# Two of four output-projection column blocks as one Strassen pass in a one-core hybrid decoder layer

## The chip, the cores and the metric

The kernel runs on one core of a Trainium2 chip. The metric is the device time of one execution in microseconds (us), lower is better. The engines are named as in the profile: PE (TensorE matmul), PEld (its weight loads), DVE (VectorE), ACT (ScalarE), POOL (GpSimd) and SP (SyncE, which here only issues DMAs). PE reads operands from SBUF and accumulates in PSUM, which has eight banks of 128 x 512 fp32.

## The reference

One decoder layer over 512 tokens of width 2048, in fp32:

```python
h = rmsnorm(x, ln_mix)
sb_q, sb_k, sb_v, sw_q, sw_k, sw_v = split(h @ w_in)
sb_o = stick_breaking_attention(sb_q, sb_k, sb_v)               # 16 heads of 64
sw_o = sliding_window_sink_attention(sw_q, sw_k, sw_v, sinks)   # 16 heads, 4 key/value heads
mixed = concat([rmsnorm(sb_o, sb_out_norm), rmsnorm(sw_o, swa_out_norm)])
x = x + mixed @ w_out                                           # 2048 x 2048
h = rmsnorm(x, ln_ffn)
gate, up = split(h @ w_gate_up)                                 # 2048 x 11264
x = x + (silu(gate) * up) @ w_down                              # 5632 x 2048
return rmsnorm(x, ln_final)
```

The change concerns the second half of `mixed @ w_out`: the 1024 columns of `sw_o`, normed, times the lower 1024 rows of `w_out`, which is 1024 x 2048.

## The kernel before

**A product in fp32.** PE multiplies in the type fp32r, so each fp32 operand is split in two: a head (`hi`, the value rounded by an ACT copy) and a rest (`lo`, value minus head, a DVE or POOL subtraction). A product is three matmuls: head x head, head x rest, rest x head. Weights come by DMA into `raw` tiles (512 KB, three buffers, `wp`), ACT makes `whi` and DVE `wlo`, two buffers each.

**The slab queue.** Plain products wait in a list, `queue`. An entry is a slab of weights with the steps that use it; a step is one trio of matmuls (128 x 128 weights, 512 columns each in the output projection). `step()` runs the next one; at the third step of a slab it asks for the loads of the next two slabs and the split of the next one (`split`, L205). `pull(ns)` runs steps for a nominal time, `drain(mark)` runs them up to a place in the queue, and `defer(n, fn)` calls `fn` after `n` steps. `add_tok` (L370) queues a product with tokens on the output partitions: four slabs of 256 rows, each with 2 x 4 steps, into four PSUM banks, one for each of four token tiles.

**The Strassen passes.** `Block` (L490) does a 2 x 2 block product with seven products instead of eight, in the order `PD`. Each product has two parts of 256 rows, and one part (a slot) is 12 matmuls of 512 columns (`product`, L508). The sums on the weight side are POOL subtractions (`difference`), the sums on the left side are `form`s. For a slot, ACT makes the head twice: `hi` in SBUF for PE, and `hp` in PSUM, which DVE reads to make `lo`. `take` (L523) adds a finished bank into the accumulators on DVE. What is done in which slot stands in a table, `plan`, filled by `at_slot(n, stage, fn)` and emptied by `run(n, stage)`. `ValuePass` (L598) does the projection of `sb_v` in this way in 28 slots, with a prologue in slots -6 to -1 that runs beside the last steps of an earlier product. The feed-forward part uses the same scheme.

**Order.** Engines take their instructions in the order in which the planner of the language emits them: mostly program order, with unpinned instructions moved where the planner finds a gap. `pV`, `pA`, `pG`, `pT` and `dma` are pinned, that is, they keep program order. An instruction waits by semaphores for what it reads and for the buffers that it writes.

**Around the change.** The sliding-window stage (L1069 to L1180) runs 16 jobs (four head groups of four token blocks): scores, exponentials, transposes (`swa_tr`), and the product with the values (`swa_av`). Its PE work is mixed with steps of the queue, which holds the last input projections and then `add_outA(0..3)`, the first half of the output projection. At the last block of a group, `swa_av` squares the outputs `oB` on ACT and POOL adds them into `sqB` (L1153). `drain()` (L1181) empties the queue; `sumsq_rstd` (L732) makes `rstdB`, the factor of each token. Then `add_outB(0..3)` (L1258) queues the second half: four column blocks of 512, each 32 steps, into banks `four(1)`, which are the two `m` banks and the two `o` banks. Its left side is `mixB`, made by `mix_split` (L1040), which scales `oB` by the norm weight (`gcol`) and splits it. At the end of a block, `done` adds the bank times `rstdB` into `x2[c]`, stores it, and defers `h2_split(c)` (L1199): 16 PE transposes and the scaling of the feed-forward's input `xh`. After block 1 all seven `form`s of the first half of `xh` are made in one deferred call (L1269), on DVE, ACT and, for one sum, POOL. The feed-forward part starts with `start_unit` (L1726), which makes the forms of the second half.

Of the kernel before, what the change touches and what calls it, by code (L numbers as in the profile page):

```python
# [37 lines left out]
def tile_hymba(ctx: ExitStack, tc: tile.TileContext, x, ln_mix, w_in, sb_norm, swa_norm,  # L38
# [39 lines left out]
    def po():  # L78
        return bank("o", 2)
# [645 lines left out]
    def sumsq_add(acc, o, first, t):  # L725
        if first:
            A.activation(out=acc, in_=o, func=AF.Square)
        else:
            A.activation(out=t, in_=o, func=AF.Square)  # L729
            G.tensor_tensor(out=acc, in0=acc, in1=t, op=ALU.add)  # L730

    def sumsq_rstd(acc, name):  # L732
        pb = po()
        for t in range(NT):
            mm(pb[:, 2 * t:2 * t + 2], lhsT=acc[:, t * P:(t + 1) * P], rhs=ones[:, 0:2],
               start=(t == 0), stop=True, skip_group_check=True)
# [265 lines left out]
    sqB = swp.tile([P, 512], F32, name="sqB", bufs=1)
    oB = [swp.tile([P, 4, 512], F32, tag="oB", name="oB", bufs=2) for _ in range(2)]
# [135 lines left out]
    def swa_av(g, blk):  # L1139
        B = blks[(g, blk)]  # L1140
        nk = B.nk
        ob = pz()
        for j in range(nk):
            vb = swv[0][:, blk - nk + 1 + j, g, :]
            mm(ob, lhsT=vb, rhs=B.p[j][0], start=(j == 0), stop=False)
            mm(ob, lhsT=vb, rhs=B.p[j][1], start=False, stop=(j == nk - 1))
# [12 lines left out]
    pull(2600.0)  # L1159
    at(swa_scores, 0)  # L1160
    stacks = {0: lambda: stack_queries(1, 0), 1: lambda: stack_queries(1, 1), 2: lambda: stack_keys(0, 1),
              5: lambda: stack_keys(1, 0), 6: lambda: stack_keys(1, 1)}
    for j in range(NJ + 2):
        at(swa_exp, j)
        if j == 3:
            rstdA = sumsq_rstd(sqA, "rstdA")
        if j in stacks:
            stacks[j]()
        pull(SWFILL / 4)
        at(swa_tr, j - 1)  # L1170
        pull(SWFILL / 4)
# [5 lines left out]
        pull(SWFILL / 4)  # L1177
        at(swa_norm, j)
        at(swa_scores, j + 1)
        pull(SWFILL / 4)  # L1180
# [45 lines left out]
    def form(p, s, parts="+hl"):  # L1226


        eV, eA = (pV, pA) if s and p not in "17" else (V, A)
        xa, xb = xh[2 * s], xh[2 * s + 1]  # L1230
        a11, a21 = xa[:, :, 0:256], xa[:, :, 256:512]
        if p not in "17":
            a12, a22 = xb[:, :, 0:256], xb[:, :, 256:512]
        if "+" in parts:
            if p == "7":
                src = e8("s3")[:, 0:2, :].rearrange("p u (a b) -> p (u a) b", a=2)
                V.tensor_tensor(out=src, in0=a11, in1=a21, op=ALU.subtract)
            elif p == "5":
                src = a21
                eV.tensor_tensor(out=src, in0=a21, in1=a22, op=ALU.add)  # L1240
            elif p == "6":
                src = a11
                eV.tensor_tensor(out=src, in0=a21, in1=a11, op=ALU.subtract)
            elif p == "3":
                src = a12
                (pG if s else G).tensor_tensor(out=src, in0=a12, in1=a11, op=ALU.subtract)
            else:
                src = {"1": lambda: a11, "2": lambda: a12, "4": lambda: a22}[p]()
            fsrc[p, s] = src
        src = fsrc[p, s]  # L1250
        if "h" in parts:
            hc[p, s] = form_tile(p, s)
            eA.activation(out=hc[p, s][:, :, 0:256], in_=src, func=AF.Copy)
        if "l" in parts:
            hl = hc[p, s]
            eV.tensor_tensor(out=hl[:, :, 256:512], in0=src, in1=f(hl)[:, :, 0:256], op=ALU.subtract)

    def add_outB(c):  # L1258
        def done(t, pb):
            xc = x2[c][:, t, :]  # L1260
            V.scalar_tensor_tensor(out=xc, in0=pb, scalar=rstdB[:, t:t + 1], in1=xc, op0=ALU.mult, op1=ALU.add)
            if t == NT - 1:
                if c < 3:
                    dma(out=x2s[c], in_=x2[c])
                    defer(6, lambda: h2_split(c))
                else:
                    nc.scalar.dma_start(out=x2s[c], in_=x2[c])
                if c == 1:
                    defer(12, lambda: [form(p, 0) for p in PR])  # L1269
                if c == 2:  # L1270
                    defer(12, lambda: [form(p, 1) for p in "17"])
            if c < 3:
                A.activation(out=junk, in_=xc, func=AF.Square, accum_out=ss2[:, t, c:c + 1])
# [12 lines left out]
    r2 = {}

# [585 lines left out]
```

## Time and profile before

| what | value |
|---|---|
| median of 3 runs | 1988.39 us (1988.22 to 1989.09) |
| the profiled execution | 1988.84 us |
| its span (first to last instruction) | 1987.0 us |
| instructions | 28973 |
| DVE, ACT, POOL busy | 1480.3, 1498.5, 999.8 us |
| queue of SP: bytes, share of 16 DMA engines | 244.11 MB, 42.2% |
| HBM, mean over the span | 120 GB/s |

A page of the profile gives the busy time of each engine. Other views give the chain of work that ended last, groups of instructions by line, the instructions of one engine in order of time, and the busy time in chosen stretches. In a row of the timeline the first number is the start in us from the span's start, the second the duration, "x4" the number of merged instructions, and a bracket at the end the idle time of the engine before it with what ended it. The end of a matmul is modelled, so that consecutive matmuls overlap in these rows; their pace is seen from start to start. The 1.84 us between span and time lie outside the instructions.

### The profile page before, as it was taken

How to read it: one execution, taken by the hardware profiler on the slowest of the kernel's cores; microseconds unless marked ns; L12 is line 12 of the kernel's file. 1: busy time of each engine (PE TensorE's matmuls, PEld its weight loads, DVE VectorE, ACT ScalarE, POOL GpSimd, SP SyncE). 2: the span in 40 equal slices, each digit the busy share in tenths (PEclk: the TensorE clock that was granted, in tenths of full speed). 3: DMA queues.
4: the chain of work that ended last, by engine and by line, in shares of the span. 5: the costliest groups of instructions: out<-in, count | busy, mean ns of one | idle time of the engine just before them, and what ended most of it. 6: DMA issues, size and time to landing. Idle time of an engine off the chain costs nothing.

```text
span 1987.0 us, 28973 instructions
## 1 busy us (share of the span) xinstructions
PE 1974.1 (99%) x10204; PEld 1687.7 (85%) x10204; DVE 1480.3 (75%) x2053; ACT 1498.5 (75%) x2015; POOL 999.8 (50%) x441
## 2 busy tenths in 40 slices
PE   9999999999999999999999999999999999999998
PEld 8888888898888888888888888888888888888886
DVE  6676888889964787777777777777777867767767
ACT  6775878868753587777777777777777788888887
POOL 2840000000010266657576666657575778878883
PEclk9999999999999999999999999999999999999999
DMA  6415454422342554444545354444534734433523
GB/s 203 148 54 142 97 144 113 121 75 85 96 138 96 172 136 113 127 125 114 137 103 144 101 139 110 129 121 118 135 104 129 279 127 148 149 127 120 177 75 117
DMA packets 290977, 252.81 MB, mean 127 GB/s; under 512 B 12560, under 2 KB 234832, under 8 KB 288400
## 3 DMA queue, kind: packets, MB, share of 16 engines
q1 hardware_dynamic: 289072, 244.11, 42.2%
q0 software_dynamic: 1376, 5.52, 0.9%
q8 instruction: 81, 1.33, 0.3%
q10 hardware_dynamic: 384, 1.34, 0.2%
q14 instruction: 64, 0.52, 0.1%
HBM read 218.40 MB, written 19.92 MB: 120 GB/s over the span
## 4 chain that ended last, share of the span: by engine, by line
PE 97%; ACT 2%; DVE 1%; issue 0%; DVEq 0%; POOL 0%; ACTq 0%; POOLq 0%
PE o L118 36%; PE m L118 30%; PE m L418 3%; PE m L419 3%; PE m L420 3%; PE m L384 2%; PE m L382 2%; PE m L383 2%; PE z L118 1%; PE o L384 1%; PE o L382 1%; PE o L383 1%; PE z L933 1%; PE o L961 1%; PE z L1132 1%; PE z L886 1%
## 5 line engine op out<-in xcount | busy, mean ns | idle before, releaser
L118 DVE TENSOR_TENSOR wlo<-t,hp 128x1024 fp32r<-128x1024 f32 x247 | 301.2, 1219 | 184.6 <-PE o L118 114.2
L118 POOL TENSOR_TENSOR t<-raw,t 128x1024 f32<-128x1024 f32 x111 | 282.2, 2543 | 281.5 <-ACT hp L118 269.6
L118 ACT ACTIVATE whi<-t 128x1024 fp32r<-128x1024 f32 x247 | 262.1, 1061 | 126.4 <-PE o L118 76.4
L118 PE MATMUL o<-hca,whi 128*128 128x512 f32 x880 | 307.5, 391 | 0.0
L118 POOL TENSOR_TENSOR t<-raw,raw 128x1024 f32<-128x1024 f32 x114 | 295.0, 2590 | 21.9 <-issue 11.3
L118 DVE TENSOR_TENSOR wlo<-raw,hp 128x1024 fp32r<-128x1024 f32 x187 | 228.3, 1221 | 93.2 <-issue 52.2
L118 ACT ACTIVATE whi<-raw 128x1024 fp32r<-128x1024 f32 (+1 forms) x189 | 200.0, 1058 | 105.0 <-PE m L118 75.0
L118 ACT ACTIVATE hp<-t 128x1024 fp32r<-128x1024 f32 x247 | 249.2, 1009 | 2.9 <-POOL t L118 2.9
L118 PE MATMUL o<-hca,wlo 128*128 128x256 f32 x880 | 244.0, 280 | 0.0
L118 ACT ACTIVATE hp<-raw 128x1024 fp32r<-128x1024 f32 x191 | 192.9, 1010 | 3.8 <-DVE wlo L118 1.4
L118 PEld LDWEIGHTS o<-hca,whi 128*128 128x128 f32 x880 | 164.2, 187 | 35.8
L118 PE MATMUL m<-hca,whi 128*128 128x512 f32 x528 | 186.3, 392 | 1.1 <-DVE hca L118 1.1
L118 PEld LDWEIGHTS o<-hca,wlo 128*128 128x128 f32 x880 | 165.6, 189 | 0.4
L221 ACT ACTIVATE whi<-raw 128x1024 fp32r<-128x1024 f32 x87 | 91.9, 1057 | 86.1 <-PE o L384 38.6
L222 DVE TENSOR_TENSOR wlo<-raw,whi 128x1024 fp32r<-128x1024 f32 x87 | 109.4, 1258 | 54.7 <-ACT whi L221 52.6
L730 POOL TENSOR_TENSOR sqA<-sqA,oc 128x512 f32<-128x512 f32 x7 | 10.1, 1439 | 273.9 <-ACT oc L729 273.9
L118 PE MATMUL m<-whi,dca 128*128 128x512 f32 x592 | 146.9, 389 | 0.0
L118 PE MATMUL o<-whi,dca 128*128 128x512 f32 x592 | 146.8, 389 | 0.0
L118 PE MATMUL m<-hca,wlo 128*128 128x256 f32 x528 | 146.3, 280 | 0.0
L118 PEld LDWEIGHTS o<-whi,dca 128*128 128x128 f32 x592 | 111.1, 188 | 23.0
L118 PEld LDWEIGHTS m<-whi,dca 128*128 128x128 f32 x592 | 111.0, 188 | 23.1
L118 PE MATMUL m<-hcs,whi 128*128 128x512 f32 x352 | 125.9, 392 | 0.0
(364 smaller groups left out, 5187.5 us busy)
## 6 DMA issues: line engine op xcount, KB each, us to landing
raw<-in_w_gate_up_dram SPq DMA_DIRECT2D x348, 256.0 KB, 5.2
raw<-in_w_down_dram SPq DMA_DIRECT2D x68, 512.0 KB, 5.0
raw<-in_w_in_dram SPq DMA_DIRECT2D x35, 512.0 KB, 4.5
raw<-in_w_in_dram SPq DMA_DIRECT2D x66, 256.0 KB, 3.9
raw<-in_w_out_dram SPq DMA_DIRECT2D x32, 512.0 KB, 3.7
aT<-w SPq DMA_DIRECT2D x44, 256.0 KB, 3.4
xd<-aT SPq DMA_DIRECT2D x10, 1024.0 KB, 6.7
rx<-in_w_down_dram SPq DMA_DIRECT2D x20, 512.0 KB, 5.7
```

Of the source, the lines that this page charges most:

```text
L118: return lambda *a, **k: tc.keep_in_program_order(fn(*a, **k))
L221: A.activation(out=hi, in_=raw, func=AF.Copy)
L222: V.tensor_tensor(out=lo, in0=raw, in1=f(hi), op=ALU.subtract)
L382: mm(o, lhsT=lh[:, sl], rhs=hi[:, j, :], start=first, stop=False, skip_group_check=halves)
L383: mm(o, lhsT=lh[:, sl], rhs=lo[:, j, :], start=False, stop=False, skip_group_check=halves)
L384: mm(o, lhsT=ll[:, sl], rhs=hi[:, j, :], start=False, stop=(k == nslab * a - 1), skip_group_check=halves)
L418: mm(o, lhsT=wh, rhs=xh, start=(k == 0), stop=False)
L419: mm(o, lhsT=wh, rhs=xl, start=False, stop=False)
L420: mm(o, lhsT=wl, rhs=xh, start=False, stop=(k == KT - 1))
L886: mm(out, lhsT=kb, rhs=H.q2[:, c0:S], start=False, stop=True, skip_group_check=True)
L933: mm(zb[:, o:o + r.shape[1]], lhsT=lhsT, rhs=r, start=False, stop=last, skip_group_check=True)
L961: mm(H.ob[:, c0:S], lhsT=vb, rhs=r[:, o:o + S - c0], start=(k == 3 and r is B.h), stop=(k == 0 and r is B.l), skip_group_check=True)
```

## The change

Column blocks 0 and 1 of the second half are now one Strassen pass, `OutPass`, of 14 slots; blocks 2 and 3 stay plain. In detail:

- `swa_av` scales `oB` in place by the norm weight on ACT, after the squares, and `mix_split` is no longer used there. `split_b` makes heads and rests of `oB` in four parts, in slots -6 to -3.
- `oB` and `sqB` move to other pools, so that the stage's work tiles can be given up before the pass.
- The last three slabs of `add_outA(3)` (24 steps) are held back (`a_end - 3`) and run four in each of the slots -6 to -1. `sumsq_rstd` stands in slot -4 and uses a `z` bank.
- The pass loads each quadrant of its weights in two parts. POOL makes the sums on the weight side; on the left side form 7's sum is POOL's, those of forms 5, 6 and 3 are DVE's; the rest of form 7 is DVE's, the others POOL's.
- `take` and `add_u` scale by `rstd_b` while they add into `x2`.
- During blocks 2 and 3 the transposes for blocks 0 and 1, their stores, their sums of squares and the forms of the first half of `xh` are deferred one at a time; several of these forms move from DVE to POOL.

```diff
+    obp = obs.enter_context(tc.tile_pool(name="obp", bufs=1))
+    oB = [obp.tile([P, 4, 512], F32, name=f"oB{n}") for n in range(2)]
     swp = open_phase("swp", 15)
-    sqB = swp.tile([P, 512], F32, name="sqB", bufs=1)
-    oB = [swp.tile([P, 4, 512], F32, tag="oB", name="oB", bufs=2) for _ in range(2)]
+    sqB = const.tile([P, S], F32, tag="rbc2", name="sqB")
...
+    def split_b(m, e):
+        if e == 0:
+            mixB[8 + m] = (act8("mhi"), act8("mlo"))
+        hi, lo = mixB[8 + m]
+        pA.activation(out=hi[:, e:e + 2, :], in_=oB[m][:, e:e + 2, :], func=AF.Copy)
+        pV.tensor_tensor(out=lo[:, e:e + 2, :], in0=oB[m][:, e:e + 2, :], in1=f(hi)[:, e:e + 2, :], op=ALU.subtract)
...
         if blk == NT - 1:
             for j in range(2):
-                sumsq_add(sqB, oB[g // 2][:, (g % 2) * 2 + j, :], g == 0 and j == 0, tmp(name="oc"))
+                o = oB[g // 2][:, (g % 2) * 2 + j, :]
+                sumsq_add(sqB, o, g == 0 and j == 0, tmp(name="oc"))
+                A.activation(out=o, in_=o, func=AF.Copy, scale=gcol[:, 40 + 2 * g + j:41 + 2 * g + j])
...
-    drain()
+    drain(a_end - 3)
     kqs.close()
-    rstdB = sumsq_rstd(sqB, "rstdB")
+    class OutPass(Block):
+        def __init__(self):
+            Block.__init__(self, 0, 0, 0, [], "6")
...
+        def add(self, p, eng):
+            b = self.block
+            if p == "7":
+                self.s3 = self.tile("t", [P, 2, 512], bufs=3).rearrange("p u (a b) -> p (u a) b", a=2)
+                eng.tensor_tensor(out=self.s3, in0=b("11"), in1=b("21"), op=ALU.subtract)
+            elif p == "5":
+                eng.tensor_tensor(out=b("21"), in0=b("21"), in1=b("22"), op=ALU.add)
+            elif p == "6":
+                eng.tensor_tensor(out=b("11"), in0=b("21"), in1=b("11"), op=ALU.subtract)
+            else:
+                eng.tensor_tensor(out=b("12"), in0=b("12"), in1=b("11"), op=ALU.subtract)
...
+    for k, q, i in ((-6, "22", 0), (-6, "12", 0), (-5, "11", 0), (-4, "11", 1), (-3, "12", 1), (-2, "22", 1),
+                    (0, "21", 0), (1, "21", 1)):
+        at_slot(k, "load", bp.load, q, i)
+    for k, fn, *args in ((-5, bp.add, "7", pG), (-4, bp.sum, "7", 0), (-3, bp.sum, "5", 0),
+                         (-2, bp.form, "7", pV), (-1, bp.sum, "6", 0), (-1, bp.add, "3", pV),
+                         (0, bp.sum, "7", 1), (1, bp.sum, "5", 1), (2, bp.form, "6", pG), (3, bp.sum, "6", 1),
+                         (4, bp.sum, "4", 0), (5, bp.sum, "4", 1), (6, bp.form, "5", pG), (8, bp.form, "3", pG)):
+        at_slot(k, "sum", fn, *args)
+    for k in range(4):
+        at_slot(k - 6, "late", split_b, k // 2, k % 2 * 2)
+    for k, p in ((-4, "7"), (0, "6"), (4, "5"), (7, "3")):
+        at_slot(k, "late", bp.form, p)
+    at_slot(-3, "late", bp.add, "5", pV)
+    at_slot(-2, "late", bp.add, "6", pV)
...
+    def b_slot(n):
+        run(n, "load")
+        run(n, "sum")
+        bof(n + 1, "to_hi")
+        bof(n + 1, "to_lo")
+        bof(n + 2, "to_hp")
+
+    for n in range(-6, 0):
+        if n == -4:
+            rstd_b.append(sumsq_rstd(sqB, "rstdB", pz()))
+        if n == -2:
+            open_z("psb")
+        b_slot(n)
+        for _ in range(4):
+            step()
+        run(n, "late")
...
-                if c == 1:
-                    defer(12, lambda: [form(p, 0) for p in PR])
...
-    add_outB(0)
-    outB0 = len(queue)
-    for c in range(1, 4):
+    for c in (2, 3):
         add_outB(c)
-    drain(outB0)
+    for n in range(14):
+        b_slot(n)
+        if n == 9:
+            load(a_end)
+        if n == 12:
+            load(a_end + 1)
+        if n == 13:
+            split(a_end)
+        bof(n, "product")
+        run(n, "take")
+        run(n, "late")
+    run(14, "take")
...
+    steps = ((2, lambda: h2_split(0)), (3, lambda: dma(out=x2s[0], in_=x2[0])), (4, lambda: form("7", 0, "+")),
+             (5, lambda: form("1", 0, "h")), (7, lambda: form("1", 0, "l")), (8, lambda: h2_split(1)),
...
+             (24, lambda: form("6", 0, "h")), (26, lambda: form("6", 0, "l")), (28, lambda: form("3", 0, "h")),
+             (30, lambda: form("3", 0, "l")))
+    for k, fn in steps:
+        defer(k, fn)
+    for k in range(8):
+        defer(4 + 3 * k, lambda k=k: norm_sums(k // 4, k % 4))
```

More of the change, by code (lines that the diff above doesn't have):

```diff
@@ L730, in sumsq_add, with sumsq_rstd @@
             G.tensor_tensor(out=acc, in0=acc, in1=t, op=ALU.add)
-    def sumsq_rstd(acc, name):
-        pb = po()
+    def sumsq_rstd(acc, name, pb=None):
+        pb = po() if pb is None else pb
         for t in range(NT):
@@ L998, in tile_hymba @@
     pull(6000.0, swv_end - 1)
+    phase[0].close()
+    phase[0] = None
+    obs = ExitStack()
+    obp = obs.enter_context(tc.tile_pool(name="obp", bufs=1))
+    oB = [obp.tile([P, 4, 512], F32, name=f"oB{n}") for n in range(2)]
     swp = open_phase("swp", 15)
[L1002 to L1003 removed]
+    sqB = const.tile([P, S], F32, tag="rbc2", name="sqB")
     kst = [None, None]
@@ L1050, in mix_prep @@
         return lambda s: [mix_split(mix, oX, g0, 2 * s + e) for e in range(2)]
+    def split_b(m, e):
[4 more added lines that the diff above has]
+        pV.tensor_tensor(out=lo[:, e:e + 2, :], in0=oB[m][:, e:e + 2, :], in1=f(hi)[:, e:e + 2, :], op=ALU.subtract)
+        for j in (e, e + 1):
+            mixB[4 * m + j] = (hi[:, j, :], lo[:, j, :])
     x2 = [None] * 4
@@ L1067, in tile_hymba @@
         add_outA(c)
+    a_end = len(queue)
     def swa_scores(g, blk):
@@ L1158, in tile_hymba @@
     SWFILL = 5800.0
-    pull(2600.0)
+    pull(2600.0, a_end - 3)
     at(swa_scores, 0)
@@ L1168, in tile_hymba @@
             stacks[j]()
-        pull(SWFILL / 4)
+        pull(SWFILL / 4, a_end - 3)
         at(swa_tr, j - 1)
-        pull(SWFILL / 4)
+        pull(SWFILL / 4, a_end - 3)
         if j == 2:
@@ new lines, in tile_hymba, with bof @@
+    rstd_b = []
+    open_phase("op", 1, reuse_waits="tile")
+    bp = OutPass()
+    def bof(n, what):
+        if 0 <= n < 14:
+            getattr(bp, what)((PD[n // 2], n % 2))
+    for k, q, i in ((-6, "22", 0), (-6, "12", 0), (-5, "11", 0), (-4, "11", 1), (-3, "12", 1), (-2, "22", 1),
[6 more added lines that the diff above has]
+        at_slot(k, "sum", fn, *args)
@@ new lines, in tile_hymba @@
+    for k in range(4):
[4 more added lines that the diff above has]
+    at_slot(-2, "late", bp.add, "6", pV)
+    for k, p in enumerate(PD):
+        at_slot(2 * k + 2, "take", bp.take, p)
+    for k, c, h in ((8, 1, 0), (9, 0, 2), (11, 1, 2)):
+        for t in range(2):
+            at_slot(k + t, "late", bp.add_u, c, h, t)
+    def b_slot(n):
[4 more added lines that the diff above has]
+        bof(n + 2, "to_hp")
@@ L1239, in form @@
                 src = a21
-                eV.tensor_tensor(out=src, in0=a21, in1=a22, op=ALU.add)
+                (eV if s else G).tensor_tensor(out=src, in0=a21, in1=a22, op=ALU.add)
             elif p == "6":
                 src = a11
-                eV.tensor_tensor(out=src, in0=a21, in1=a11, op=ALU.subtract)
+                (eV if s else G).tensor_tensor(out=src, in0=a21, in1=a11, op=ALU.subtract)
             elif p == "3":
@@ L1246, in form @@
                 (pG if s else G).tensor_tensor(out=src, in0=a12, in1=a11, op=ALU.subtract)
-            else:
-                src = {"1": lambda: a11, "2": lambda: a12, "4": lambda: a22}[p]()
-            fsrc[p, s] = src
+            if p not in "124":
+                fsrc[p, s] = src
+        if p in "124":
+            fsrc[p, s] = {"1": lambda: a11, "2": lambda: a12, "4": lambda: a22}[p]()
         src = fsrc[p, s]
@@ L1255, in form, with norm_sums @@
             hl = hc[p, s]
-            eV.tensor_tensor(out=hl[:, :, 256:512], in0=src, in1=f(hl)[:, :, 0:256], op=ALU.subtract)
+            (G if s == 0 and p in "243" else eV).tensor_tensor(out=hl[:, :, 256:512], in0=src, in1=f(hl)[:, :, 0:256],
+                                                                op=ALU.subtract)
+    def norm_sums(c, t):
+        A.activation(out=junk, in_=x2[c][:, t, :], func=AF.Square, accum_out=ss2[:, t, c:c + 1])
     def add_outB(c):
@@ L1260, in done @@
             xc = x2[c][:, t, :]
-            V.scalar_tensor_tensor(out=xc, in0=pb, scalar=rstdB[:, t:t + 1], in1=xc, op0=ALU.mult, op1=ALU.add)
+            V.scalar_tensor_tensor(out=xc, in0=pb, scalar=rstd_b[0][:, t:t + 1], in1=xc, op0=ALU.mult, op1=ALU.add)
             if t == NT - 1:
```

70 lines of the change are left out of this document (65 added, 5 removed).

## The prediction

> **What bounds the kernel now.** I read the page's busy shares and its chain first, then the waits of PE, and then the busy time in the stretches around the output projection.
>
> ```profile
> PE 1974.1 (99%) x10204; PEld 1687.7 (85%) x10204; DVE 1480.3 (75%) x2053; ACT 1498.5 (75%) x2015; POOL 999.8 (50%) x441
> PE 97%; ACT 2%; DVE 1%; issue 0%; DVEq 0%; POOL 0%; ACTq 0%; POOLq 0%
> PE m L118 <- DVE hca L118: 1.1, 1, 1.1
> PE o L118 <- DVE hct L118: 0.3, 1, 0.3
> ```
>
> PE is busy for 99% of the span and 97% of the chain that ended last is PE. In the middle of the kernel it waits visibly only twice, 1.1 and 0.3 us, for forms that DVE makes. So a matmul taken out is worth its pace, as long as nothing new is late. The next rows are the busy times (us and instructions of PE, PEld, DVE, ACT, POOL) of the existing value pass, of the sliding-window stage, of its tail, of the second half of the output projection, and of the feed-forward's start.
>
> ```profile
> 58.68:134.68 76.00, 76.00 (x337) 62.90 (x337) 49.80 (x54) 60.81 (x63) 54.45 (x24) 1.00 0.22 70
> 460.00:560.00 100.00, 99.75 (x516) 83.07 (x515) 94.35 (x240) 81.03 (x209) 9.10 (x8) 1.00 0.29 90
> 575.00:598.60 23.60, 23.60 (x105) 19.51 (x104) 11.57 (x13) 7.11 (x9) 4.19 (x4) 1.00 0.55 175
> 598.60:692.03 93.43, 93.43 (x441) 78.08 (x441) 56.96 (x63) 37.82 (x58) 8.08 (x4) 1.00 0.39 125
> 692.03:716.00 23.97, 22.57 (x132) 19.44 (x131) 23.16 (x24) 20.80 (x27) 15.55 (x12) 1.00 0.51 158
> ```
>
> The second half takes 93.43 us with PE never idle and POOL nearly empty (8.08 us). The value pass, which has the scheme that the change copies, also leaves PE no gap, with POOL at 54.45 of 76 us. The only stretch here in which PE loses something (1.40 of 23.97 us) has forms on DVE beside POOL work.
>
> **What the change removes.** The pace of a 512-column matmul:
>
> ```profile
> 602.32 0.39 PE L382 MATMUL o<-whi,mhi 128*128 128x512 f32 x1
> 617.96 0.39 PE L382 MATMUL m<-whi,mhi 128*128 128x512 f32 x1
> 129.40 5.44 PE o L118 x24
> ```
>
> From 602.32 to 617.96 stand 69 starts of the plain product, so 0.2267 us each; the value pass has 24 in 5.44, the same. Blocks 0 and 1 have 2 x 96 = 192 matmuls; the pass has 14 slots of 12, that is 168. Twenty-four fewer are **-5.44 us**, 0.27% of the time. The 32 transposes, eight sums of squares, two stores, eight weight loads of 512 KB and `sumsq_rstd` are only moved. The DVE and ACT work grows, but in the pass itself it has the value pass's cover: per slot (2.72 us) one rest, one `hi`, one `hp`; banks are taken every second slot.
>
> **The prologue** is the place where this gain can go. These rows are PE's end of the window stage, and ACT, POOL and DVE behind it.
>
> ```profile
> 579.37 0.40 PE L1146 MATMUL z<-plo,swv 128*128 128x512 f32 x1
> 598.64 0.95 PE L735 MATMUL o<-ones,sqB 128*128 128x2 f32 x8
> 581.30 1.15 ACT L729 ACTIVATE oc<-oB 128x512 f32<-128x512 f32 x2 [0.91 <-DVE oB L722]
> 582.09 2.99 POOL L730 TENSOR_TENSOR sqB<-sqB,oc 128x512 f32<-128x512 f32 x2 [1.48 <-ACT oc L729]
> 585.02 0.79 POOL L118 DMA_DIRECT2D x<-in_x_dram  x1
> 584.05 2.10 DVE L222 TENSOR_TENSOR wlo<-raw,whi 128x1024 fp32r<-128x1024 f32 x1
> ```
>
> After the last value product (579.6) 28 steps of 0.68 us remain; 24 are now held back, so slot -6 begins at about 582.3, and with `sumsq_rstd` (0.81 us, 598.64 to the next matmul at 599.45) the pass still begins at about 599.5. Nothing is left without filler in the window stage. The rest of product 1's first part, `lo`, is read by its ninth matmul, at 599.5 + 8 x 0.2267 = **601.3**.
>
> DVE meets that only if it gets through what stands ahead of it, since a pinned instruction does not overtake earlier work on its engine. The value pass's prologue shows that: ACT had been free for 4.45 us, the operand's head `hp` was long made, and still the pinned `whi` came behind the plain evacuation.
>
> ```profile
> 55.99 0.60 ACT L576 ACTIVATE kq<-m 128x512 f32<-128x512 f32 x1 [4.45 <-PE m L571]
> 56.49 1.05 ACT L118 ACTIVATE whi<-rx 128x1024 fp32r<-128x1024 f32 x1
> L222 DVE TENSOR_TENSOR wlo<-raw,whi 128x1024 fp32r<-128x1024 f32 x87 | 109.4, 1258 | 54.7 <-ACT whi L221 52.6 <-PE o L961 1.1
> L118 POOL TENSOR_TENSOR vf<-vs,vf 128x1024 fp32r<-128x1024 f32 x8 | 19.2, 2404 | 4.4 <-ACT vf L118 4.4
> ```
>
> From 586.0 on (the end of the rest of the slab before) DVE has ahead of that `lo`: four rests of `split_b`, the rest of the last slab, add 5, form 7's rest, add 6 and add 3, nine of at most 1.26 us; two evacuations (0.75 each, `done` below), some seven small ones of `rstdB` (I put 0.17, an estimate from that same short chain after 599.6 in the trace), and `lo` itself: 11.3 + 1.5 + 1.2 + 1.2 = 15.2, so it ends at 601.2. On DVE alone it just fits: **0**. But POOL has four instructions of 2.40 ready at the same time (form 7's sum and three weight sums), and two more when form 7's rest is done. How the two get on is in these rows:
>
> ```profile
> 658.78 2.40 POOL L1246 TENSOR_TENSOR xh<-xh 128x1024 f32<-128x1024 f32 x1 [72.97 <-DVE xh L1243]
> 658.94 3.33 DVE L222 TENSOR_TENSOR wlo<-raw,whi 128x1024 fp32r<-128x1024 f32 x1 [0.31 <-ACT whi L221]
> 707.07 2.40 POOL L118 TENSOR_TENSOR xh<-xh 128x1024 f32<-128x1024 f32 x1 [2.25 <-DVE xh L118]
> 708.16 2.38 DVE L118 TENSOR_TENSOR hca<-xh,hca 128x1024 fp32r<-128x1024 f32 x1
> 709.42 6.75 POOL L118 TENSOR_TENSOR t<-raw,raw 128x1024 f32<-128x1024 f32 x2
> 710.60 1.19 PE L118 MATMUL m<-hca,whi 128*128 128x512 f32 x4 [1.11 <-DVE hca L118]
> ```
>
> DVE's 658.94 ends 1.09 us after POOL's end at 661.18, 708.16 ends 1.08 after 709.47, and POOL's pair beside DVE takes 6.75 where 4.8 is usual. A DVE instruction with two SBUF inputs and a POOL instruction with SBUF inputs stand one behind the other. Those nine are all of that kind, while a pass's own `lo` reads `hp` from PSUM and is not. Laid end to end, 6 x 2.40 = 14.4 us come on top: the bounds are 0 and 14.4. The nearest row is the feed-forward's start, where three such POOL instructions (707.07 and the pair) stood beside forms on DVE and PE lost 1.40, that is 0.47 for each. The four that are ready at once then cost **+1.9**; the two later ones follow form 7's rest and I count them at nothing.
>
> The Trainium skill, page "SBUF — State Buffer", section "Who interferes with whom", states the rule behind these rows: a DVE instruction with two SBUF inputs and a GpSimd instruction that reads SBUF exclude each other for the whole instruction. By it the full end-to-end sum would stand; the trace agrees on each pair, and what a whole queue of such pairs costs PE no run here shows. That is the second rival.
>
> **The other places.**
>
> ```profile
> 687.73 0.39 PE L384 MATMUL m<-whi,mlo 128*128 128x512 f32 x1
> 688.15 0.75 DVE L1261 SCALAR_TENSOR_TENSOR x<-m,rstdB,x 128x512 f32<-128x512 f32 x1 [0.31 <-PE m L384]
> 551.91 1.30 PE L1132 MATMUL z<-ident,s 128*128 128x128 f32 x8
> 552.00 0.50 ACT L1122 ACTIVATE s<-s,den 128x256 f32<-128x256 f32 x1
> 517.68 0.38 PE L1132 MATMUL z<-ident,s 128*128 128x128 f32 x2
> 517.81 0.48 PE L382 MATMUL m<-whi,mhi 128*128 128x512 f32 x1
> ```
>
> *End of the pass.* Product 3 ends in the `m` banks and block 2 begins in them (`four(1)`). An evacuation starts 0.42 after its last matmul's start (687.73, 688.15), takes 0.75, and PE follows 0.06 later (708.16 + 2.38 to 710.60). Bank 0's last matmul is the one before last, so PE waits 0.42 + 0.75 + 0.06 - 0.45 = 0.78, unless the planner puts other matmuls there, as it mixed transposes and matmuls from 517.68 on. Between 0 and 0.8 I take **+0.3**, nearer to the mixed row.
>
> *Window stage.* Eight scalings on ACT (0.58 each by 581.30) come in four pairs, three of them ahead of transposes that wait on ACT (551.91 ended with the `s` of 552.00). At worst 3 x 1.15 = 3.5; at best the stage's whole loss of 0.25 goes, since eight rests of `oB` leave a DVE busy for 94.35 of 100 us. I take **+0.2**, by that row: PE lost next to nothing with bursts of this size already there.
>
> *Blocks 2 and 3.* POOL gets six form instructions (14.4 us) beside eight slab rests and five form instructions on DVE. A slab's rest ends some 2.7 us after its slab's predecessor began (a head of about one us on ACT, then 1.26) and is needed 5.44 after; one wait behind POOL is covered, as at 658.94, where PE went on; a second costs up to 2.1. Bounds 0 and, for two such cases, 4.2; I take 0. *Feed-forward's start:* its forms are unchanged, and so are its 1.40 us; bounds -1.4 and 0, I take 0.
>
> **Sum:** -5.44 + 1.9 + 0.3 + 0.2 = -3.04. The profiled execution's own 1988.84 (span 1987.0 and 1.84 around it) becomes 1985.80; it lies 0.45 above the median 1988.39, so the median becomes **1985.35**.
>
> **The rivals.**
>
> *All is hidden* (faster). POOL's operands land late, or DVE is through its rests before POOL starts, so that the prologue costs nothing: -5.44 + 0.5 = -4.9, **1983.5**. For it: the value pass's prologue ran without a gap. Against it: that one had no DVE instruction with two SBUF inputs beside POOL.
>
> *One behind the other* (slower). POOL and DVE alternate from 586 on and product 1 starts without its `lo`. Of the 14.4 us, DVE's evacuations and small work (2.7) run beside POOL, and some 0.3 of slack goes first: 11.4 late. -5.44 + 11.4 + 0.5 = +6.5, **1994.9**. It decides above 9.4 us of loss (5.44 and 0.2%), that is 1.5 us or more for each of the six POOL instructions. For it: the three pairs above. Against it: it needs POOL to have all its operands early.
>
> *The change does not do what it says* I set aside: PE's count falls by 24 whatever the order, and PE is the bound.
>
> **Chances.** About 0.2%, 3.98 us, is what a measurement of this kernel can tell from no change. Forecast, within 0.2%: 0.42, its own range 1984.4 to 1988.5. All hidden, faster by more: 0.36. One behind the other, slower by more: 0.22. For the range, 1983.2 leaves out a gain of the whole 5.44 (0.05), and 1993.6 leaves out the larger part of the last rival (0.15).
>
> **What would show it.** PE's matmul count falls by 24 and blocks 0 and 1 take 14 slots of 2.72 us. In the prologue: DVE's `lo` rows of `split_b`, add 5, add 6 and add 3 longer than 1.3 us beside POOL, and a PE wait for DVE `wlo` at about 599 to 601, of some 2 us by the forecast, of 10 by the last rival, of none by the first. At the end of the pass a PE wait of 0.8 or none for the evacuation of the `m` banks. A PE wait in the window stage of over 1 us, or in blocks 2 and 3 for a slab's rest, would show a term that I put at next to nothing wrong; so would a PE gap above 3 us at a place not named here.

## The result and the profile after

| | before | after |
|---|---|---|
| median | 1988.49 us (1988.22 to 1989.09, 4 runs) | 2002.91 us (2002.4 to 2003.73, 4 runs) |
| span of the profiled execution | 1987.0 us | 2002.0 us |
| its mean granted clock | 0.999 | 0.994 |

The ratio is 1.0072 with a 95% interval of 1.0055 to 1.009. The change made the kernel slower by 14.4 us, more than 0.2%. The forecast was 1985.35 and its range ended at 1993.6, so both were wrong.

The page of the kernel after: the line of busy times, then the chain by engine.

```profile
PE 1976.7 (99%) x10180; PEld 1688.2 (84%) x10180; DVE 1511.5 (76%) x2066; ACT 1524.3 (76%) x2043; POOL 1047.0 (52%) x458
...
PE 92%; DVE 3%; ACT 2%; issue 2%; POOL 1%; DVEq 0%; ACTq 0%; POOLq 0%
```

PE has its 24 matmuls fewer (10204 to 10180), and yet it is busy for longer, 1976.7 instead of 1974.1 us: some of its matmuls have become slower. Its share of the chain fell from 97% to 92%. The five points, about 100 us, are not the size of the loss: where this chain leaves PE at a wait, it follows the other engines back through work beside which PE ran (from 460 to 493 it is on ACT and DVE, while PE is busy for 99.65 us of the stretch 460 to 560). The waits of PE (us in total, times, longest) have four rows that were not there before:

```profile
PE m L383 <- DVE wlo L222: 6.8, 2, 4.6
PE m L118 <- DVE wlo L118: 2.9, 1, 2.9
PE m L382 <- ACT whi L221: 2.1, 1, 2.1
...
PE m L382 <- DVE x L1405: 0.6, 1, 0.6
```

These five waits lie in the prologue of the pass, in its first product and in block 2. The same is seen in the busy time by stretch (PE, PEld, DVE, ACT, POOL; then the granted clock): the prologue's last part and product 1, the rest of the pass, the end of block 2, and the window stage.

```profile
594.00:604.50 10.50, 6.20 (x16) 4.48 (x15) 9.89 (x12) 7.00 (x9) 3.99 (x3) 0.67 0.60 213
604.50:618.00 13.50, 10.63 (x35) 8.17 (x34) 10.16 (x8) 5.64 (x6) 9.03 (x4) 0.75 0.00 1
618.00:646.00 28.00, 28.00 (x125) 23.16 (x124) 21.89 (x26) 21.88 (x23) 10.17 (x5) 1.00 0.01 1
...
671.00:690.00 19.00, 13.78 (x62) 10.87 (x61) 13.44 (x11) 5.74 (x11) 9.75 (x4) 0.91 0.19 56
460.00:560.00 100.00, 99.65 (x516) 83.19 (x516) 91.72 (x231) 80.98 (x209) 9.06 (x8) 1.00 0.30 95
```

From 618 on the pass runs without a gap, and the window stage loses no more than before (99.65 busy, 99.75 before). In the first, second and fourth stretch PE is idle, and the granted clock drops too, to 0.67, 0.75 and 0.91. PE's own rows show how both come about. These are the matmuls on either side of each wait, and the last slow ones behind it.

```profile
593.91 0.39 PE L384 MATMUL o<-whi,mlo 128*128 128x512 f32 x1
596.35 0.50 PE L382 MATMUL m<-whi,mhi 128*128 128x512 f32 x1 [2.05 <-ACT whi L221]
599.10 0.80 PE L383 MATMUL m<-wlo,mhi 128*128 128x512 f32 x1 [2.25 <-DVE wlo L222]
...
604.34 0.39 PE L383 MATMUL o<-wlo,mhi 128*128 128x512 f32 x1
...
607.77 1.07 PE L118 MATMUL m<-whi,mlo 128*128 128x512 f32 x4
611.71 2.07 PE L118 MATMUL m<-wlo,mhi 128*128 128x512 f32 x4 [2.87 <-DVE wlo L118]
...
618.35 0.63 PE L118 MATMUL o<-whi,vf 128*128 128x512 f32 x2
...
671.20 0.39 PE L382 MATMUL m<-whi,mhi 128*128 128x512 f32 x1
676.19 0.80 PE L383 MATMUL m<-wlo,mhi 128*128 128x512 f32 x1 [4.60 <-DVE wlo L222]
...
679.34 0.41 PE L384 MATMUL m<-whi,mlo 128*128 128x512 f32 x1
...
682.79 0.39 PE L384 MATMUL o<-whi,mlo 128*128 128x512 f32 x1
683.81 0.47 PE L382 MATMUL m<-whi,mhi 128*128 128x512 f32 x1 [0.63 <-DVE x L1405]
```

Read them from start to start and take off the pace of 0.227. The waits cost 2.21, 2.53 (prologue), 3.03 (the first part's `lo` in product 1; the last of the four at 607.77 starts at 608.45), 4.76 and 0.79 us (block 2), 13.3 together. Behind three of them the matmuls start 0.43 apart. From 599.10 to 604.34 stand 12 starts in 5.24 us where 2.72 would do; from 611.71 to 618.35 there are 16 in 6.64, and from 676.19 to 679.34 seven in 3.15. That is 2.5, 3.0 and 1.6 us of half clock, 7.1 together. 13.3 + 7.1 - 5.44 = 15.0, the whole difference of the spans. What else moved is small beside it.

**The prologue.** DVE, POOL and ACT between 585 and 612, in the kernel after:

```profile
585.85 6.75 DVE L118 TENSOR_TENSOR mlo<-oB,mhi 128x1024 fp32r<-128x1024 f32 x2
...
592.71 2.16 DVE L278 TENSOR_SCALAR rv<-sst 128x4 f32<-128x4 f32 x1
595.38 1.92 DVE L284 TENSOR_TENSOR rt<-rr 128x4 f32<-128x4 f32 x1 [0.51 <-ACT rr L282]
...
597.82 1.23 DVE L222 TENSOR_TENSOR wlo<-raw,whi 128x1024 fp32r<-128x1024 f32 x1
...
607.78 2.74 DVE L118 TENSOR_TENSOR oB<-oB,oB 128x1024 f32<-128x1024 f32 x1
610.45 1.21 DVE L118 TENSOR_TENSOR wlo<-rx,hp 128x1024 fp32r<-128x1024 f32 x1
```

```profile
585.54 2.65 POOL L118 TENSOR_TENSOR t<-oB 128x1024 f32<-128x1024 f32 x1
588.15 3.37 POOL L118 TENSOR_TENSOR t<-raw,raw 128x1024 f32<-128x1024 f32 x1
591.60 3.25 POOL L118 TENSOR_TENSOR raw<-raw,rx 128x1024 f32<-128x1024 f32 x1
594.93 2.36 POOL L118 TENSOR_TENSOR t<-raw,raw 128x1024 f32<-128x1024 f32 x1
```

```profile
594.91 0.20 ACT L280 ACTIVATE rl<-rv 128x4 f32<-128x4 f32 x1 [8.34 <-DVE rv L278]
595.15 0.20 ACT L282 ACTIVATE rr<-rl 128x4 f32<-128x4 f32 x1
595.26 1.04 ACT L221 ACTIVATE whi<-raw 128x1024 fp32r<-128x1024 f32 x1
```

POOL's four instructions start at 585.54 and run almost without a break to 597.29. In that time DVE gets two rests through (6.75 us instead of 2.4) and three tiny instructions, two of which are held for 2.16 and 1.92 us: `rv` ends with POOL's third instruction (594.85), `rt` with the fourth (597.29). ACT's logarithm waits for `rv`, and behind that logarithm, in program order, stands the head of the last held-back slab (595.26). So the 2.21 us for `whi` go back to four numbers for each partition that DVE could not get done, and before them to the two rests, which were held as well. The slab's rest follows at 597.82, and product 1's `lo` ends at 611.66, 10.4 us after the 601.3 at which the forecast has PE read it. The half clock ahead of it (2.5 us) only shortens the wait for it; the 3.0 behind it come on top: 10.4 + 3.0 = 13.4, against 2.21 + 2.53 + 2.5 + 3.03 + 3.0 = 13.3 counted on PE.

**Blocks 2 and 3.** POOL and DVE at the end of block 2:

```profile
662.63 3.31 POOL L1379 TENSOR_TENSOR xh<-xh 128x1024 f32<-128x1024 f32 x1 [25.86 <-DVE xh L1353]
666.02 2.41 POOL L1382 TENSOR_TENSOR xh<-xh 128x1024 f32<-128x1024 f32 x1
668.38 3.39 POOL L1396 TENSOR_TENSOR hcs<-xh,hcs 128x1024 fp32r<-128x1024 f32 x1
671.74 3.32 POOL L1396 TENSOR_TENSOR hca<-xh,hca 128x1024 fp32r<-128x1024 f32 x1
675.02 3.34 POOL L1385 TENSOR_TENSOR xh<-xh 128x1024 f32<-128x1024 f32 x1
```

```profile
667.07 5.79 DVE L1396 TENSOR_TENSOR hca<-xh,hca 128x1024 fp32r<-128x1024 f32 x2 [3.38 <-ACT hca L1393]
672.78 3.35 DVE L222 TENSOR_TENSOR wlo<-raw,whi 128x1024 fp32r<-128x1024 f32 x1
680.43 2.57 DVE L222 TENSOR_TENSOR wlo<-raw,whi 128x1024 fp32r<-128x1024 f32 x1 [4.29 <-ACT whi L221]
```

The forms were asked for one by one, yet they came in a bunch, since all wait for `xh`, which is complete at 662.6. POOL then has five without a pause. Each DVE instruction with two SBUF inputs waits for the end of one of them: two rests of forms take 5.79 us, and the slab's rest behind them ends at 676.13, where PE had been waiting since 671.4. The next one (680.43) delays an evacuation, hence the last 0.79.

### The profile page after: what moved, and what is told of

It reads as the page before. It is cut to its first block, busy times and chain, and to the rows that moved or that the text cites. A ratio compares the mean times of both kernels' runs of the same rounds, so it can differ in the third digit from the quotient of the medians.

```text
span 2002.0 us, 29013 instructions
## 1 busy us (share of the span) xinstructions
PE 1976.7 (99%) x10180; PEld 1688.2 (84%) x10180; DVE 1511.5 (76%) x2066; ACT 1524.3 (76%) x2043; POOL 1047.0 (52%) x458
## 4 chain that ended last, share of the span: by engine, by line
PE 92%; DVE 3%; ACT 2%; issue 2%; POOL 1%; DVEq 0%; ACTq 0%; POOLq 0%
PE o L118 37%; PE m L118 31%; PE m L418 3%; PE m L419 3%; PE m L420 3%; PE z L118 1%; PE z L933 1%; PE m L382 1%; PE m L383 1%; PE m L384 1%; PE o L961 1%; PE o L383 1%; PE o L384 1%; PE o L382 1%; PE z L1146 1%
## 5 line engine op out<-in xcount | busy, mean ns | idle before, releaser
L118 DVE TENSOR_TENSOR wlo<-t,hp 128x1024 fp32r<-128x1024 f32 x253 | 308.4, 1219 | 191.2 <-PE o L118 115.5
L118 ACT ACTIVATE whi<-t 128x1024 fp32r<-128x1024 f32 x253 | 268.5, 1061 | 130.0 <-PE o L118 78.3
L118 POOL TENSOR_TENSOR t<-raw,raw 128x1024 f32<-128x1024 f32 x118 | 305.9, 2596 | 29.4 <-issue 11.7
L118 DVE TENSOR_TENSOR wlo<-raw,hp 128x1024 fp32r<-128x1024 f32 x191 | 233.2, 1221 | 92.9 <-issue 51.6
L118 ACT ACTIVATE whi<-raw 128x1024 fp32r<-128x1024 f32 (+1 forms) x193 | 204.1, 1058 | 107.4 <-PE m L118 75.2
L118 ACT ACTIVATE hp<-t 128x1024 fp32r<-128x1024 f32 x253 | 255.2, 1009 | 8.0 <-POOL t L118 4.3
L222 DVE TENSOR_TENSOR wlo<-raw,whi 128x1024 fp32r<-128x1024 f32 x79 | 100.2, 1268 | 35.6 <-ACT whi L221 34.1
L418 PE MATMUL m<-hhi,whi 128*128 128x512 f32 x320 | 125.8, 393 | 0.0
```

The lines of the kernel that those rows point to most:

```text
L118: return lambda *a, **k: tc.keep_in_program_order(fn(*a, **k))
L222: V.tensor_tensor(out=lo, in0=raw, in1=f(hi), op=ALU.subtract)
L418: mm(o, lhsT=wh, rhs=xh, start=(k == 0), stop=False)
```

## The experiments

The theory: DVE and POOL hold each other up in two places, and PE pays once for waiting and once more for the half clock behind it. The rivals: DVE has too much to do whoever does the sums; the order on ACT or on DVE alone is the fault; the half clock comes from load and not from idleness.

**1. The forms of blocks 2 and 3 on DVE.**

```diff
-                (eV if s else G).tensor_tensor(out=src, in0=a21, in1=a22, op=ALU.add)
+                eV.tensor_tensor(out=src, in0=a21, in1=a22, op=ALU.add)
...
-                (eV if s else G).tensor_tensor(out=src, in0=a21, in1=a11, op=ALU.subtract)
+                eV.tensor_tensor(out=src, in0=a21, in1=a11, op=ALU.subtract)
...
-            (G if s == 0 and p in "243" else eV).tensor_tensor(out=hl[:, :, 256:512], in0=src, in1=f(hl)[:, :, 0:256],
+            eV.tensor_tensor(out=hl[:, :, 256:512], in0=src, in1=f(hl)[:, :, 0:256],
```

> The changed kernel with the sums 5 and 6 and the rests of forms 2, 4 and 3 of the feed-forward's first half (blocks 2 and 3) on DVE instead of POOL; nothing else. Theory (in blocks 2 and 3 the slab rest on DVE stands behind a row of POOL instructions, 2.4 us each, and PE then pays twice, the wait and half clock after it): the waits at 671 and 683 (4.76 and 0.79 us) and the slow matmuls after the first (1.6 us) go, so about 7 us less than the changed kernel, 1996. Rival (DVE is simply overloaded there; five more instructions of 1.22 us on it make the slab rest later still): the wait at 671 stays or grows, time 2003 or more.

Measured: 1995.15 us (1994.64 to 1996.21, 5 runs), ratio to before 1.0032 (1.0019 to 1.0045), 7.8 less than after. The busy time in the stretch where PE had stood still:

```profile
664.00:675.00 11.00, 11.00 (x50) 8.94 (x49) 11.00 (x9) 4.80 (x6) 3.28 (x1) 1.00 0.06 23
```

DVE is busy for all of the 11 us, and PE loses nothing. Five more instructions on DVE cost nothing; the same five on POOL cost PE 7 us. The rival falls. Whether the slab's rest ahead of the two rests of forms would have been enough, no run shows.

**2. The token factors one slot later.**

```diff
-        if n == -4:
+        if n == -3:
             rstd_b.append(sumsq_rstd(sqB, "rstdB", pz()))
```

> The changed kernel with sumsq_rstd asked for one slot later (-3 instead of -4), so that its Ln and Exp on ACT and its small DVE work no longer stand ahead of the split of the last held-back slab. Theory A (DVE and POOL together have too much to do ahead of product 1's lo, whatever the order): the waits at 594 and 596 (2.21 and 2.53 us, with about 2.5 us of half clock behind them) shrink or go, but PE then comes earlier to lo, which ends at 611 as before, and waits there for 8 to 10 us: total within 3 us of the changed kernel, 2000 to 2003. Theory B (the order on ACT is the cause, the load is not): 4.7 us of waits and 2.5 us of half clock go and nothing new comes, 1995.7.

Measured: 2002.32 us (1.0069, 1.0056 to 1.0081), 0.6 less than after. The wait for `whi` is gone and that for the slab's rest fell to 1.70. In their place PE waits 2.83 for the evacuation of the `m` banks and 3.73 for `lo`, with half clock behind each. That is not the 8 to 10 us for `lo` alone that theory A had named, but its time holds: the order on ACT decided where PE waited, and hardly how long.

**3. The prologue's four early POOL instructions on DVE.**

```diff
-    for k, fn, *args in ((-5, bp.add, "7", pG), (-4, bp.sum, "7", 0), (-3, bp.sum, "5", 0),
+    for k, fn, *args in ((-5, bp.add, "7", pV), (-4, bp.sum, "7", 0), (-3, bp.sum, "5", 0),
...
             self.difference(p, i, self.raw["12", i] if p == "5" else self.t["6", i] if p == "4" else
-                            self.tile("t", [P, 2, 512], bufs=3))
+                            self.tile("t", [P, 2, 512], bufs=3), pV if p in "756" and i == 0 else pG)
```

> The changed kernel with the four POOL instructions of the prologue before product 1 (form 7's sum, first parts of the weight sums of products 7, 5 and 6) on DVE in the same places; the later ones stay on POOL. Theory (POOL and DVE exclude each other, so a sum costs DVE 2.4 us or more while POOL has it and 1.22 if DVE does it itself): DVE has 13 instructions of 1.22, two evacuations and small work, 18.6 us from 585.9, so lo ends at about 604.5 instead of 611.65; PE loses about 3 us there instead of 7.8, and little to half clock: about 8 to 10 us less than the changed kernel, 1993 to 1995. Rival (they do not exclude each other, or the loads that land at 590 to 597 set the pace): four more instructions on DVE make lo later by up to 4.9 us, 2003 to 2009.

Measured: 1999.52 us (1.0053, 1.0041 to 1.0066), 3.4 less than after. The direction is the theory's, the size less than half of it. DVE's timeline tells why:

```profile
589.02 0.17 DVE L278 TENSOR_SCALAR rv<-sst 128x4 f32<-128x4 f32 x1
...
597.20 1.22 DVE L118 TENSOR_TENSOR vf<-t,vf 128x1024 fp32r<-128x1024 f32 x1
...
599.65 2.38 DVE L118 TENSOR_TENSOR oB<-oB 128x1024 f32<-128x1024 f32 x1
601.96 3.35 DVE L118 TENSOR_TENSOR t<-raw,raw 128x1024 f32<-128x1024 f32 x1
```

With POOL silent, every instruction up to 598.4 takes its bare time: 1.22, and `rv` 0.17 instead of 2.16. DVE is through form 7's rest 5 us earlier than in the kernel after, though it did three instructions more (the fourth, the weight sum of product 6, is the row at 601.96). PE does not wait before product 1. Then POOL's two later sums begin (598.56 and 601.02), DVE pays 1.16 and 2.13 us beside them, and `lo`, behind that, ends at 607.58. PE's one wait is 6.12 us.

**4. Five waits put into the kernel before.**

```diff
             A.activation(out=hi, in_=raw, func=AF.Copy)
+            late = {1: 3, 4: 4, 7: 5, 10: 6, 13: 9}.get(i - outB[0], 0) if outB else 0
+            for _ in range(late):
+                A.activation(out=hi, in_=f(hi), func=AF.Copy)
             V.tensor_tensor(out=lo, in0=raw, in1=f(hi), op=ALU.subtract)
+            if late:
+                A.activation(out=hi, in_=f(hi), func=AF.Copy)
```

> The kernel before, with five deliberate PE waits in the second half of the output projection: the head of slabs 1, 4, 7, 10 and 13 is copied onto itself 3, 4, 5, 6 and 9 more times by ACT (1.05 us each) before its rest is made and once after it, so that PE stands idle for about 1.6, 2.6, 3.7, 4.7 and 7.9 us and then can run on. Theory (a PE wait beyond some length lowers the granted clock to half for 3 to 6 us, at 0.2 us for each matmul, with nothing else needed): matmuls start 0.427 us apart after the longer waits and 0.227 after the shortest, and the time grows by the waits (about 20 us) and 1.5 to 3 us for each long one. Rival (the half clock in the changed kernel came from load on SBUF, DMA or from POOL beside it): 0.227 after every wait, and the time grows by the waits alone.

Measured: 2021.05 us (one run). The waits, from start to start, were 0.54, 1.73, 3.67, 9.24 and 9.22 us, not the ones aimed at. The busy time just behind the second, the third and the fourth, with PE's matmuls counted:

```profile
626.10:632.00 5.90, 5.90 (x27) 4.86 (x28) 5.80 (x7) 2.76 (x5) 0.00 (x0) 1.00 0.69 210
...
646.00:652.00 6.00, 5.91 (x14) 4.66 (x15) 1.22 (x3) 0.76 (x3) 0.00 (x0) 0.50 0.00 0
...
676.30:679.30 3.00, 2.94 (x7) 2.36 (x8) 0.05 (x1) 0.01 (x1) 0.00 (x0) 0.50 0.53 173
```

After 0.54 and 1.73 us PE went on at full pace. After the three longer waits it had a granted clock of 0.50 and cost 2.9, 1.5 and 2.4 us more, with POOL idle in these rows (0.00) and DMA at nothing or at half. So idleness is enough, and the price does not grow with the wait: the longest had less than that of 3.67.

**5. All together.** The edits of experiments 1 and 3, and what product 1 does not need goes behind its `lo`:

```diff
-                         (-2, bp.form, "7", pV), (-1, bp.sum, "6", 0), (-1, bp.add, "3", pV),
-                         (0, bp.sum, "7", 1), (1, bp.sum, "5", 1), (2, bp.form, "6", pG), (3, bp.sum, "6", 1),
+                         (-2, bp.form, "7", pV), (4, bp.add, "3", pV),
+                         (0, bp.sum, "7", 1), (1, bp.sum, "5", 1), (2, bp.sum, "6", 0), (2, bp.form, "6", pG), (3, bp.sum, "6", 1),
...
-    for k, p in ((-4, "7"), (0, "6"), (4, "5"), (7, "3")):
+    for k, p in ((-4, "7"), (1, "6"), (4, "5"), (7, "3")):
...
-    at_slot(-2, "late", bp.add, "6", pV)
+    at_slot(0, "late", bp.add, "6", pV)
```

> The changed kernel with the forms of blocks 2 and 3 on DVE (as in e1_forms_dve), the four early POOL instructions of the prologue on DVE (as in e3_sums_dve), and what product 1 does not need taken from ahead of its lo: add 6, add 3 and the first part of the weight sum of product 6 go to slots 0, 4 and 2. In e3_sums_dve DVE was through form 7's rest at 598.4 with every instruction at 1.22, and only then two POOL sums stretched add 6 and that weight sum to 2.38 and 3.35. Theory (these places hold the whole loss, 20.4 us with the half clock): lo ends at about 600, before PE needs it, no wait of PE between 585 and 700 over 1 us, and the time is the changed kernel's less about 19 to 20, 1983 to 1984, faster than the kernel before by 4.5 to 5.5. Rival (the 24 matmuls are paid for elsewhere too, or the moved instructions make products 7 or 6 late): a new wait of PE between 600 and 615, or a time above 1987.

Measured: 1987.73 us (1985.76 to 1989.98, 11 runs), ratio to before 0.9995 (0.9986 to 1.0004). Of the loss 15.2 us are gone, but the expectation is missed by 4 and the time can't be told from that of the kernel before. Both signs of the rival are there, a time above 1987 and a wait of PE, which ends at 601.29; its cause is the rest of form 7 on DVE:

```profile
597.07 3.41 DVE L118 TENSOR_TENSOR vf<-t,vf 128x1024 fp32r<-128x1024 f32 x1
```

It ran into the first of POOL's later sums (596.86 to 599.40). Behind it stood the evacuation of the `m` banks, for which PE waited 2.27 us, with 1.6 us of half clock after it.

**6. Only the order of that run,** on the kernel after: the edit just shown, and nothing of experiments 1 and 3.

> The changed kernel with only the order of that run: add 6, add 3 and the weight sum of product 6 go behind product 1's lo (slots 0, 4 and 2); every instruction stays on its engine, POOL keeps its sums, blocks 2 and 3 are as in the changed kernel. If the order of the prologue alone were the fault, PE's waits there would all go: 1990. If POOL beside DVE and the ACT order behind it are the fault, the waits at 594 and 596 (4.7 us with half clock behind) stay, as nothing ahead of them moves; only the wait for lo (3.03 us and about 3 us of half clock) goes: 1997 to 1999, with the wait at 671 as before.

Measured: 1999.56 us (1.0054, 1.0042 to 1.0067), 3.4 less than after. The wait for `lo` went, the 2.21 for `whi` and the 4.75 in block 2 stayed, as they should if POOL beside DVE is the fault. The wait for the slab's rest did not stay: it fell from 2.53 to 1.03. The expectation had overlooked that the edit takes POOL's fourth instruction away from beside `rt`, which now took 0.16 instead of 1.92. The half clock behind these two waits stayed (2.8 us). The time missed the expectation by half a microsecond, since waits of 1.58 for the evacuation of the `m` banks and of 0.78 at product 4's start had not been counted.

**7. Form 7's rest behind the second `lo`.**

```diff
-                         (-2, bp.form, "7", pV), (4, bp.add, "3", pV),
+                         (4, bp.add, "3", pV),
...
-    for k, p in ((-4, "7"), (1, "6"), (4, "5"), (7, "3")):
+    for k, p in ((-4, "7"), (4, "5"), (7, "3")):
...
-    at_slot(0, "late", bp.add, "6", pV)
+    at_slot(0, "late", bp.form, "7", pV)
+    at_slot(1, "late", bp.add, "6", pV)
+    at_slot(1, "late", bp.form, "6")
```

> e5_all_moved with one thing more: form 7's rest goes from slot -2 to slot 0, behind product 1's second lo, and add 6 with form 6's head from slot 0 to slot 1. In e5_all_moved that rest ran at 597.07 beside a POOL sum, took 3.41 instead of 1.22, and the evacuation of the m banks stood behind it: PE waited 2.27 us at 599 and paid some 2.2 us of half clock. Theory: that wait and its half clock go and no other comes (nothing with two SBUF inputs is left on DVE between the landing of the last weights and the evacuation), 1983 to 1984, 0.25 to 0.3% faster than the kernel before. Rival (the locked rest only moves and now makes product 7 late, or the second lo): a new wait of PE of 2 us or more between 600 and 607, 1986 to 1989.

Measured: 1985.69 us (1985.37 to 1986.96, 11 runs), ratio to before 0.9985 (0.9976 to 0.9994), faster than before but about 2 us short of the expectation. The wait at 599 and its half clock went. At 616, a place that neither side had named, PE waited 1.42 us for the head of product 4's first slot. Its POOL sum stood behind two other POOL instructions and took 3.39 us itself.

**8. That sum on DVE.** (The expectation calls the slot that waited the second; by the order of PE's matmuls it is product 4's first.)

```diff
-                            self.tile("t", [P, 2, 512], bufs=3), pV if p in "756" and i == 0 else pG)
+                            self.tile("t", [P, 2, 512], bufs=3), pV if i == 0 else pG)
...
-                         (4, bp.add, "3", pV),
+                         (6, bp.add, "3", pV),
```

> e7_rest_later with the first part of product 4's weight sum on DVE instead of POOL, and add 3 from slot 4 to slot 6. In e7_rest_later PE waited 1.42 us at 616 for the head of product 4's second slot, which waits for that POOL sum behind three others. Theory: the sum is done at about 612.5 instead of 614.3, that wait goes, and the time falls by 1 to 1.5 us to about 1984.5, all but 1 us of what the 24 matmuls are worth. Rival (the lock only moves, to the rests of slots 4 to 6): a wait of PE for DVE wlo between 610 and 620, 1986 or more.

Measured: 1984.37 us (1983.77 to 1985.22, 11 runs) against 1989.05, ratio 0.9977 (0.9968 to 0.9986). This version beats both kernels, the one before by 4.7 us. The stretches that had gaps in the kernel after:

```profile
594.00:604.50 10.50, 10.50 (x48) 8.71 (x47) 10.50 (x12) 6.01 (x7) 5.13 (x2) 1.00 0.51 187
604.50:618.00 13.50, 13.09 (x57) 10.00 (x56) 13.38 (x13) 10.57 (x11) 9.02 (x4) 1.00 0.00 0
```

48 matmuls instead of 16 in the first, and a clock of 1.00. Between 585 and 760 PE's gaps beyond its pace, those over 0.15 us each, are 2.65 us (before: 1.91), between 430 and 585 they are 0.85 (before: 1.12). So -5.44 + 0.74 - 0.27 = -4.97, and with the gaps from 0.1 us on -4.65; its span, 1982.1, is 4.9 below that of before. The worth of the 24 matmuls is shown.

**9. PE kept at work through a wait.** The product of sixteen more matmuls is used by nobody.

```diff
+    def awake():
+        pb = pz()
+        for _ in range(16):
+            mm(pb, lhsT=mixB[0][0][:, 0:P], rhs=mixB[0][0], start=True, stop=True)
+
+    defer(24, awake)
```

> The changed kernel with sixteen more matmuls of 512 columns on PE, whose result nobody reads, put exactly where PE waits 4.76 us for a slab's rest at 671, ahead of the one matmul before that wait; nothing else. They take 16 x 0.227 = 3.6 us of that wait. Theory (it is PE's idleness that lowers the clock): the wait shrinks to about 1.1 us, the matmuls behind it start 0.227 apart, and the kernel with more matmuls is faster than the changed kernel by the half clock of that place, 1.6 us: about 2001.3. Rival (the clock falls because of what runs beside): the matmuls behind stay at 0.427, and the time is that of the changed kernel, 2002.9, or more.

Measured: 2003.53 us (1.0073, 1.006 to 1.0085), no gain. The rows of PE, and then one of its waits:

```profile
674.15 0.39 PE L382 MATMUL m<-whi,mhi 128*128 128x512 f32 x1
675.55 0.50 PE L383 MATMUL m<-wlo,mhi 128*128 128x512 f32 x1 [1.01 <-DVE wlo L222]
675.89 0.39 PE L384 MATMUL m<-whi,mlo 128*128 128x512 f32 x1
```

```profile
PE m L382 <- DVE x L1405: 2.1, 1, 2.1
```

On the clock the theory holds: the wait fell from 4.76 to 1.18 us, and the matmuls behind it go at full pace. On the time it fails: PE came to the next evacuation 1.5 us earlier, and that evacuation, behind the slab's rest that POOL delays, ended when it had ended before. The wait grew from 0.79 to 2.30.

## Why the prediction was wrong, step by step

- **The 24 matmuls, -5.44: right.** The sum over the gaps closes with it in the kernel after (15.0) and in the best version (-4.97).
- **The prologue, +1.9: wrong; it cost 13.3.** The step that failed is the price of 0.47 us for each of four POOL instructions, taken from PE's 1.40 us at the feed-forward's start, "the nearest row". Only two DVE instructions of the held kind stood beside POOL there. One is the 708.16 of the prediction (2.38), the other this one of the kernel before:

```profile
712.20 1.70 DVE L118 TENSOR_TENSOR hct<-xh,hct 128x1024 fp32r<-128x1024 f32 x1
```

They were held for 1.16 and 0.48 us, and PE lost nearly all of it. So the row was small because little collided, and it is no price for a POOL instruction. In the prologue nine such DVE instructions and the chain of `rstdB` stood in a row. What had to be priced was their delay, against the slack of this place, which the same paragraph had found to be next to nothing (601.2 against 601.3). The four early POOL instructions held DVE for some 8.1 us: 4.4 for the two rests of `split_b` and 3.7 for the chain of `rstdB`, against experiment 3. With the two later ones `lo` came 10.4 us late; the second rival had said 11.4. Its mechanism, POOL and DVE one behind the other, is what happened, in its place and almost in its size, and the forecast gave it 0.22. Its time, 1994.9, is still 8 us short: it too had nothing for blocks 2 and 3 and for the half clock.

- **"the two later ones follow form 7's rest and I count them at nothing": wrong.** In the kernel after, POOL's two later instructions held add 6 and add 3 for 1.10 and 1.52 us. Experiment 3 shows them alone: 1.16 and 2.13 us on DVE ahead of `lo`. In experiment 5 one of them cost PE 2.27 and half clock.
- **"DVE's evacuations and small work (2.7) run beside POOL": half wrong.** The evacuations do (1.40 to 1.45 for two). Two of the small instructions were held for 2.16 and 1.92, and through ACT's queue they held up a slab's head, of which the prediction had nothing.
- **The rule of the Trainium skill** (page "SBUF — State Buffer", section "Who interferes with whom"), by which the full sum would stand, decided rightly where the nearest row decided wrongly. The same section counts tensor_scalar among the instructions that can take the shared port; `rv`, 2.16 us beside POOL and 0.17 without, agrees.
- **Blocks 2 and 3, 0: wrong; they cost 7.1** (4.76, 0.79 and 1.6 of half clock). The bound was 4.2, for two waits of a slab's rest. The step took a first collision of each rest as covered and put the second at nothing. But POOL's instructions came five in a row, and two rests of forms stood ahead of the slab's rest in DVE's queue, each waiting for an end of POOL's. Experiment 1, which takes five of the six from POOL, is 7.8 us faster.
- **The half clock: not in the prediction at all.** 7.1 us of slow matmuls; but by experiment 9 the 1.6 in block 2 would have been a wait otherwise, and by the times in the prologue the first 2.5 as well. What it added on its own is the 3.0 behind `lo`.
- **Window stage +0.2, end of the pass +0.3, feed-forward's start 0: right within 0.3.** The first is at 99.65 of 100, at the second PE did not wait (the planner put transposes there), the third has the same two waits, 1.1 and 0.3.
- **"All is hidden", 1983.5,** needed another kernel: with the sums on DVE and the order changed, 1984.37.

Put together: -5.44 + 10.4 + 3.0 + 7.1 = 15.1, against 15.0 measured.

## What to carry to other kernels

Where an instruction moves to an engine that holds up a busy one, as POOL does DVE here, add up both queues end to end and set the result against the slack of that place; a loss seen elsewhere tells how much collided there, and is no price for an instruction. Give the work to the engine that does it in half the time, even if it is the fuller one: DVE's 1.22 us replaced 2.40 of POOL in which DVE could do little. And put what is needed first at the head of an in-order queue, ahead of every instruction that can be held up.

## What the runs showed of the hardware that was not expected

- **Half clock after waits of PE.** After waits of 0.54, 1.58, 1.70 and 1.73 us there was none. Near 2.3 it went either way: 2.27 brought it (experiment 5), 2.30 did not (experiment 9). Waits of 2.21 and 1.03 with one matmul between them brought it too (experiment 6). After 2.83, 3.03, 3.67 and all longer ones PE ran at half clock for a time that cost up to 3.0 us, in no order of the wait's length (9.24: 1.5; 3.67: 2.9). In experiment 5 it set in as late as 1.7 us after PE had started again, and in experiment 1, behind a wait of 3.82, after 1.6. The Trainium skill, page "TensorE: Matmul & The Clock Gate", section "Part 1: The HAM clock gate (the "warmup" mystery)", ascribes this to windows of about 3.4 us that run freely; the uneven prices agree. The wait of 2.27 is shorter than its idle window and was enough all the same.
- **Keeping PE busy keeps its clock.** Sixteen matmuls for nothing, put into a wait, held it at 1.00, which here only fed the next wait.
- **A held DVE instruction is held however small it is.** 128 x 4 elements took 2.16 us beside POOL's 128 x 1024, and ended as that did; without it they took 0.17.
